# Two heads' inputs kept with zeros beside them, so that the state-space output products use the whole array

## The chip, the cores and the metric

The kernel runs on one core of one Trainium2 chip. The metric is the device time of one execution in microseconds (us). PE is TensorE, whose weight loads have a track of their own (PEld); DVE is VectorE, ACT is ScalarE, POOL is GpSimd, and SP issues the DMAs.

## The reference

Two layers of an encoder trunk over 512 tokens of width 1024 are computed, in float32. Each layer has three mixers on one projection, a gated sum of them, an output projection and an MLP. What the change touches is the state-space mixer (16 heads of 64 columns, 4 chunks of 128 tokens, one scan per direction):

```python
cb = jnp.einsum('bclgn,bcsgn->bcgls', Cm, Bm)
y_diag = jnp.einsum('bcghls,bcsghp->bclghp', cb[:, :, :, None] * decay, xdt)
w_state = jnp.exp(a_last[:, :, None] - a_cum)
states = jnp.einsum('bclgn,bclghp->bcghpn', Bm, xdt * w_state[..., None])
...
y_off = jnp.einsum('bclgn,bcghpn->bclghp', Cm, s_prev) * jnp.exp(a_cum)[..., None]
return (y_diag + y_off).reshape(Bsz, S, H, P)
```

The change is in `y_diag`: for each head and chunk, a 128x128 matrix of decays times the 128 tokens' 64 inputs. Both directions share one matrix M in the kernel, since their triangles are added first.

## The kernel before

The work runs through stages, each with its own buffers: norm (F), neighbourhood attention (N), gated linear attention (G), state space (S), and the MLP in the next F. Nearly all of PE's work is the large projections: `feat` makes one 128x512 output from 24 matmuls (lines 304 to 306: weights and inputs are each split in a high and a low part, three products for each of 8 blocks). Its output lies in one of two PSUM banks (`mm`, shown as `pf`), so a third `feat` starts only when the first one's bank has been read: by L592 (`gate`), L606 (`branch`), L777 (`conv_tile`) or L957 (`gate_tile`), all on DVE.

The G stage has float32 products of 256 columns, some written alone (L731) and some added to what an earlier product wrote (L748).

The S stage treats the 16 heads in 8 pairs. For a pair, `pair_prep` transposes the inputs (L880), copies them to `xt` (L882, ACT), weights them (L887, POOL) and builds the two heads' matrices M: two rows of sums are broadcast by DMA (`S_E`, `S_eB`), DVE takes their minimum (L898, four instructions a head), ACT takes the exponential (L903), DVE adds the two triangles (L904) and multiplies (L905). `pair_states` makes the states (L916, L922, L923). `pair_out` makes the output products `py` (L933), and adds them to the inputs (L934) with the states' part (L944, L945, POOL L947).

In `pair_out` each of the 4 chunks has two products, one for each head: 128 tokens contracted, 64 output rows, 128 output columns. Head 0 writes partitions 0 to 63 of `py`, head 1 partitions 64 to 127. A float32 product like this shows as two matmul instructions in the trace, so a pair has 16 and both layers have 256.

Between the pairs' steps, `fill` puts projections of other branches (convolutions, gates, branch outputs) in program order. The order on each engine is then set by a scheduler that plans with modelled times; it also moves single products away from their neighbours. Each engine runs its own instructions in that order.

Of the kernel before, what the change touches and what calls it, by code (L numbers as in the profile page):

```python
# [11 lines left out]
AF = mybir.ActivationFunctionType  # L12
# [4 lines left out]
P = 128  # L17
NT = 512
# [181 lines left out]
def trunk(tc, a, out, layers=L, dbg=None):  # L200
    nc = tc.nc
    V, S, G, T = nc.vector, nc.scalar, nc.gpsimd, nc.tensor
    with ExitStack() as ctx:
# [29 lines left out]
        def flat(ap):  # L233
            return ap.rearrange("p a b -> p (a b)")
# [20 lines left out]
        ph = Phase(tc, "F0", F_SB, F_PS)  # L255
# [41 lines left out]
        def feat(l, key, rh, rl, ps=None):  # L297

            hi, lo = wget(l, key)
            if ps is None:  # L300
                ps = psm("pf")
            for k in range(KT):
                c = slice(P * k, P * (k + 1))
                T.matmul(ps, lhsT=hi[:, c], rhs=rh[k], start=k == 0, stop=False)  # L304
                T.matmul(ps, lhsT=hi[:, c], rhs=rl[k], start=False, stop=False)  # L305
                T.matmul(ps, lhsT=lo[:, c], rhs=rh[k], start=False, stop=k == KT - 1)  # L306
            return ps
# [74 lines left out]
        for l in range(layers):  # L382
# [36 lines left out]
            if l:  # L419
                for j in range(KT):  # L420
# [5 lines left out]
            ph = Phase(tc, f"N{l}", {"s": 5, "pT": 4, "va": 2, "vb": 2, "bias": 5, "qA": 2, "qB": 2, "v": 2,  # L426
                                     "kA": 2, "kB": 2, "lA0": 1, "lA1": 1, "lB0": 1, "lB1": 1, "ebc": 1},
                       {"sc": 2, "pt": 2, "po": 1, "v": 1})
# [11 lines left out]
            for t in range(8):  # L440
                ps = feat(l, ("nk", t), xh, xl)
# [27 lines left out]
            for t in range(8):  # L469
                ps = ph.p("sc")  # L470
# [117 lines left out]
            def gate(b, j):  # L588
                ps = feat(l, ("gate", b, j), xh, xl)
                g_ = evac("gl")  # L590
                with hp():
                    V.tensor_tensor(g_, ps, rbc, ALU.mult)  # L592
                with hp():
                    S.activation(g_, g_, AF.Tanh, scale=0.5)
                return g_

            def branch(b, j, bh, bl, g_=None):
# [9 lines left out]
                if b:  # L607
# [4 lines left out]
            ph = Phase(tc, f"G{l}", {"A": 1, "kwT": 2, "st0": (3, 256), "st1": (3, 256), "t1": 3, "t2": 3, "w": 2,  # L612
                                     "gvg": 8, "bs": 2, "gst": 1, "q": 1, "k": 1, "a2": (2, 256), "kx": (2, 256)},
                       {"ga": 1, "at": 1, "x": 2, "po": 2})
            ps = feat(l, ("sm", 0), xh, xl)
# [181 lines left out]
            for h in range(1, 4):  # L797
                y = gla_mix(h, *cur)
                if h < 3:
# [4 lines left out]
            ph.close()  # L804


            ph = Phase(tc, f"S{l}", {"xt": 2, "bt": 1, "gs": 1, "xw": (2, 768), "st": (2, 768), "eb": 4, "E": 4, "eB": 2,
                                     "T": 2, "tb": 1, "sm": 2, "xs": 4, "bc": 1, "tm": (1, 256)},
                       {"x": 4, "py": 2})

# [28 lines left out]
            for d in range(2):  # L839
                r = slice(16 * d, 16 * d + 16)  # L840
# [19 lines left out]
            def ssd_group(g, t6):  # L860
# [11 lines left out]
                    V.copy_predicated(zt[d], trim[d], ps)  # L872
                return bt

            def pair_prep(g, j, t6):

                x_, r0 = t6[j], 8 * g + 2 * j
                ps = ph.p("x", (P, 4, P))
                for c in range(4):
                    T.transpose(ps[:, c], x_[:, P * c: P * (c + 1)], ident)  # L880
                xt = ph.t("xt", (P, 4, P))
                S.activation(xt, ps, AF.Copy)  # L882
                xw = ph.t("xw", (P, 2, 3, P))
                h2 = lambda ap: ap.rearrange("p c (h e) -> p c h e", h=2)
                for d in range(2):
                    w_ = wst[:, d: d + 3, 16 * d + r0: 16 * d + r0 + 2]
                    G.tensor_tensor(h2(xw[:, d]), h2(xt[:, d: d + 3]), w_.unsqueeze(3).to_broadcast((P, 3, 2, 64)),  # L887
                                    ALU.mult)
                M = []
                for hh in range(2):  # L890
                    rf, rb = r0 + hh, 16 + r0 + hh

                    ef, eb_ = ph.t("E", (P, 4, P)), ph.t("eB", (P, 4, P))
                    nc.sync.dma_start(flat(ef), acd[rf: rf + 1, :].to_broadcast((P, NT)))
                    nc.sync.dma_start(flat(eb_), acd[rb: rb + 1, :].to_broadcast((P, NT)))
                    t_, tb = ph.t("T", (P, 4, P)), ph.t("tb", (P, 4, P))
                    for c in range(4):
                        V.scalar_tensor_tensor(ef[:, c], ef[:, c], wj[:, c, rf: rf + 1], eb_[:, c], ALU.subtract, ALU.min)  # L898
                    for c in range(4):
                        S.activation(t_[:, c], zt[0][:, c], AF.Copy, scale=dt[:, c, rf: rf + 1])  # L900
                        S.activation(tb[:, c], zt[1][:, c], AF.Copy, scale=dt[:, c, rb: rb + 1])
                    for c in range(4):
                        S.activation(ef[:, c], ef[:, c], AF.Exp, bias=nab[:, c, rf: rf + 1])  # L903
                    V.tensor_tensor(t_, t_, tb, ALU.add)  # L904
                    V.tensor_tensor(ef, ef, t_, ALU.mult)  # L905
                    M.append(ef)
                return xt, xw, M

            def pair_states(g, j, bt, xw):

                r0 = 8 * g + 2 * j
                st = ph.t("st", (P, 6, P))
                for d in range(2):
                    ps = ph.p("x", (P, 3, P))
                    for c in range(3):
                        T.matmul(ps[:, c], lhsT=bt[:, d + c], rhs=xw[:, d, c], start=True, stop=True)  # L916
                    S.activation(st[:, 3 * d: 3 * d + 3], ps, AF.Copy)
                he = lambda ap: ap.rearrange("p d (h e) -> p d h e", h=2)
                for n, prev, cur in ((0, st[:, 0::5], st[:, 1:5:3]), (1, st[:, 1:5:3], st[:, 2:4])):
                    tm = ph.t("tm", (P, 2, P))  # L920
                    de = dec[:, n].rearrange("p (d h) -> p d h", d=2)[:, :, r0: r0 + 2]
                    V.tensor_tensor(he(tm), he(prev), de.unsqueeze(3).to_broadcast((P, 2, 2, 64)), ALU.mult)  # L922
                    V.tensor_tensor(cur, cur, tm, ALU.add)  # L923
                return st

            def pair_out(g, j, t6, xt, M, st):

                x_, Ct, r0 = t6[j], t6[5], 8 * g + 2 * j
                py = ph.p("py", (P, 4, P))
                for c in range(4):  # L930
                    for hh in range(2):
                        r = slice(64 * hh, 64 * hh + 64)
                        T.matmul(py[r, c], lhsT=xt[:, c, r], rhs=M[hh][:, c], start=True, stop=True)  # L933
                V.scalar_tensor_tensor(x_, x_, cc(C_D + 4 * g + j), flat(py), ALU.mult, ALU.add)  # L934
                for d in range(2):
                    eb = ph.t("eb", (P, 3, P))
                    for hh in range(2):
                        r = 16 * d + r0 + hh
                        nc.sync.dma_start(flat(eb[64 * hh: 64 * hh + 64]),
                                          ead[r: r + 1, P - P * d: NT - P * d].to_broadcast((64, 3 * P)))  # L940
                    ps = ph.p("x", (P, 3, P))
                    for c in range(3):
                        co = c + 1 - d
                        T.matmul(ps[:, c], lhsT=st[:, 3 * d + c], rhs=Ct[:, P * co: P * (co + 1)], start=True, stop=True)  # L944
                    V.tensor_tensor(eb, ps, eb, ALU.mult)  # L945
                    xo = x_[:, P - P * d: NT - P * d]
                    G.tensor_tensor(xo, xo, flat(eb), ALU.add)  # L947
# [46 lines left out]
            pairs = [(g, j) for g in range(2) for j in range(4)]  # L994
            bts, cs = [ssd_group(0, c0)], [c0, c1]
            cur = pair_prep(0, 0, c0)
            fill(2)
            st = pair_states(0, 0, bts[0], cur[1])
            for n, (g, j) in enumerate(pairs):
# [8 lines left out]
                if nxt:  # L1008
                    st = pair_states(*nxt, bts[nxt[0]], new[1])
# [9 lines left out]
            gs = [gate(2, j) for j in range(5)]  # L1019
# [6 lines left out]
            ph = Phase(tc, f"F{l + 1}", F_SB, F_PS)  # L1026
# [6 lines left out]
            for j in range(8):  # L1033
                ps = feat(l, ("wo", j), mh, ml, ph.p("pf"))
# [4 lines left out]
            for q in range(4):  # L1039
                hh_, hl_ = [], []  # L1040
                for i in range(8):
                    ps = feat(l, ("f1", 8 * q + i), xh, xl, ph.p("pf"))
# [6 lines left out]
                for j in range(8):  # L1049
                    ps = feat(l, ("f2", q, j), hh_, hl_, ph.p("pf"))  # L1050
# [23 lines left out]
```

## Time and profile before

| | |
|---|---|
| median of 3 runs | 2468.46 us (2467.49 to 2468.6) |
| the profiled execution | 2469.9 us |
| its span, first to last instruction | 2468.1 us |
| PE busy | 2452.2 us (99%) |
| DVE busy | 1425.8 us (58%) |
| ACT busy | 1162.1 us (47%) |
| POOL busy | 393.3 us (16%) |
| granted TensorE clock, mean | 0.998 |

The profiled execution took 1.8 us more than its span, and 1.4 us more than the median. A busy PE means that some matmul was in the pipeline, so its share doesn't tell how fast the matmuls follow each other; that is read from their start times.

### The profile page before, as it was taken

Reading aid. Unit: us, or ns where it says so; the run is one execution under the profiler, and the core shown is the slowest. Engines: PE = TensorE matmul, PEld = TensorE weight load, DVE = VectorE, ACT = ScalarE, POOL = GpSimd, SP = SyncE. Lnnn points to the kernel's source line nnn. Section 1 sums busy time; section 2 is a strip of 40 time slices with the busy share of each in tenths; the row PEclk is TensorE's granted clock in tenths of the full one; section 3 lists DMA queues with packets and bytes.
Section 4 is the critical chain, followed back from the end, with each engine's and each line's share of the span. In section 5 each row is a group of like instructions: output and inputs, shape, how many; then the busy total and the mean of one; then the engine's idle time right before and its main releaser. Section 6 shows DMA issues by size and latency. Waiting matters only on the chain.

```text
span 2468.1 us, 32626 instructions
## 1 busy us (share of the span) xinstructions
PE 2452.2 (99%) x12656; PEld 2064.9 (84%) x12656; DVE 1425.8 (58%) x2148; ACT 1162.1 (47%) x2055; POOL 393.3 (16%) x333
## 2 busy tenths in 40 slices
PE   8999999999999999999999999999999999999999
PEld 7888889988788888888888888899878888888887
DVE  6776534587976554444447755345889665434443
ACT  4575435555855342332335654255568543422321
POOL 3132101112431110000122221011124312100000
PEclk9999999999999999999999999999999999999999
DMA  5221222223533322322332222222245333222232
GB/s 185 94 88 61 89 94 79 69 69 119 178 116 120 99 97 94 98 99 94 124 128 94 82 72 79 94 71 78 77 129 168 108 128 101 96 94 96 93 103 86
DMA packets 84603, 249.38 MB, mean 101 GB/s; under 512 B 9824, under 2 KB 15840, under 8 KB 84448
## 3 DMA queue, kind: packets, MB, share of 16 engines
q1 hardware_dynamic: 84016, 246.85, 30.5%
q8 instruction: 100, 1.64, 0.3%
q14 instruction: 55, 0.45, 0.1%
q10 hardware_dynamic: 432, 0.45, 0.1%
HBM read 242.80 MB, written 4.46 MB: 100 GB/s over the span
## 4 chain that ended last, share of the span: by engine, by line
PE 96%; DMA 2%; DVE 1%; ACT 1%; issue 0%; SPq 0%; DVEq 0%
PE pf L304 14%; PE pf L305 14%; PE pf L306 14%; PE F_pf L306 11%; PE F_pf L305 11%; PE F_pf L304 11%; PE pt L322 3%; PE pt L321 2%; PE pt L323 2%; PE N_po L569 2%; PE N_pt L562 1%; PE S_x L944 1%; PE G_at L699 1%; PE S_py L933 1%; PE G_at L700 1%; PE S_x L916 1%
## 5 line engine op out<-in xcount | busy, mean ns | idle before, releaser
L285 ACT ACTIVATE wh<-wr 128x1024 fp32r<-128x1024 f32 x378 | 400.2, 1059 | 938.7 <-PE F_pf L305 429.7
L287 DVE TENSOR_TENSOR wl<-wr,wh 128x1024 fp32r<-128x1024 f32 x378 | 485.7, 1285 | 188.4 <-ACT wh L285 186.6
L304 PE MATMUL pf<-xh,wh 128*128 128x512 f32 x1232 | 486.2, 395 | 7.6 <-DVE gl L592 3.7
L305 PE MATMUL pf<-xl,wh 128*128 128x512 f32 x1232 | 486.6, 395 | 0.7 <-DVE xl L349 0.7
L306 PE MATMUL pf<-xh,wl 128*128 128x512 f32 x1232 | 486.2, 395 | 0.0
L304 PEld LDWEIGHTS pf<-xh,wh 128*128 128x128 f32 x1232 | 232.2, 189 | 57.0 <-DVE gl L592 4.6
L306 PEld LDWEIGHTS pf<-xh,wl 128*128 128x128 f32 x1232 | 232.3, 189 | 49.5 <-issue 1.5
L305 PEld LDWEIGHTS pf<-xl,wh 128*128 128x128 f32 x1232 | 232.4, 189 | 48.9 <-issue 1.2
L304 PE MATMUL F_pf<-Ah,wh 128*128 128x512 f32 x640 | 248.4, 389 | 0.0
L306 PE MATMUL F_pf<-Ah,wl 128*128 128x512 f32 x640 | 247.8, 389 | 0.0
L305 PE MATMUL F_pf<-Al,wh 128*128 128x512 f32 x640 | 247.8, 389 | 0.0
L306 PE MATMUL F_pf<-xh,wl 128*128 128x512 f32 x512 | 200.1, 391 | 0.0
L305 PE MATMUL F_pf<-xl,wh 128*128 128x512 f32 x512 | 199.3, 389 | 0.0
L304 PE MATMUL F_pf<-xh,wh 128*128 128x512 f32 x512 | 199.3, 389 | 0.0
L1051 DVE TENSOR_TENSOR F_x<-F_x,F_pf 128x512 f32<-128x512 f32 x64 | 44.0, 688 | 205.6 <-PE F_pf L306 205.6
L322 PE MATMUL pt<-wl,xh 128*128 128x256 f32 x512 | 146.1, 286 | 0.0
L323 PE MATMUL pt<-wh,xl 128*128 128x256 f32 x512 | 145.9, 286 | 0.0
L321 PE MATMUL pt<-wh,xh 128*128 128x256 f32 x512 | 144.9, 284 | 0.0
L304 PEld LDWEIGHTS F_pf<-Ah,wh 128*128 128x128 f32 x640 | 120.2, 188 | 25.0
L305 PEld LDWEIGHTS F_pf<-Al,wh 128*128 128x128 f32 x640 | 120.1, 188 | 25.0
L306 PEld LDWEIGHTS F_pf<-Ah,wl 128*128 128x128 f32 x640 | 120.1, 188 | 24.8
L1044 DVE SCALAR_TENSOR_TENSOR F_v<-F_pf,rx 128x512 f32<-128x512 f32 x64 | 44.1, 691 | 159.5 <-PE F_pf L306 159.5
(313 smaller groups left out, 4257.1 us busy)
## 6 DMA issues: line engine op xcount, KB each, us to landing
wr<-pk SPq DMA_DIRECT2D x378, 512.0 KB, 3.3
N_bias<-bias SPq DMA_DIRECT2D x48, 256.0 KB, 2.9
S_E<-acd SPq DMA_DIRECT2D x32, 256.0 KB, 4.3
S_eB<-acd SPq DMA_DIRECT2D x32, 256.0 KB, 3.8
S_eb<-ead SPq DMA_DIRECT2D x64, 96.0 KB, 3.5
F_x<-xt SPq DMA_DIRECT2D x15, 256.0 KB, 5.2
xd<-F_x SPq DMA_DIRECT2D x8, 256.0 KB, 2.0
F_x<-xd SPq DMA_DIRECT2D x8, 256.0 KB, 4.8
```

Of the source, the lines that this page charges most:

```text
L285: S.activation(hi, raw, AF.Copy)
L287: V.tensor_tensor(lo, raw, f(hi), ALU.subtract)
L304: T.matmul(ps, lhsT=hi[:, c], rhs=rh[k], start=k == 0, stop=False)
L305: T.matmul(ps, lhsT=hi[:, c], rhs=rl[k], start=False, stop=False)
L306: T.matmul(ps, lhsT=lo[:, c], rhs=rh[k], start=False, stop=k == KT - 1)
L321: T.matmul(o, lhsT=rh[k][:, s], rhs=hi[:, c], start=k == 0, stop=False)
L322: T.matmul(o, lhsT=rh[k][:, s], rhs=lo[:, c], start=False, stop=False)
L323: T.matmul(o, lhsT=rl[k][:, s], rhs=hi[:, c], start=False, stop=k == KT - 1)
L562: T.transpose(pt[:, i, kb], s[:, i, P * kb: P * (kb + 1)], ident)
L569: T.matmul(po[r, P * cb: P * (cb + 1)], lhsT=vv[:, v0 + kb, r], rhs=ptS[:, i, kb], start=kb == 0, stop=kb == 1)
L1044: V.scalar_tensor_tensor(v_, ps, 0.0, rbc, ALU.max, ALU.mult)
L1051: V.tensor_tensor(xT[j], xT[j], ps, ALU.add)
```

## The change

The inputs of a pair no longer lie as 4 blocks of 128 columns (64 of head 0, 64 of head 1). Two fixed buffers of 1152 columns are set to zero once per layer, and the copy from PSUM writes head 0 to columns 128c to 128c+63 and head 1 to columns 576+128c to 576+128c+63 of chunk c. A slice of 128 columns from 128c is then head 0 with 64 columns of zeros behind it, and one from 512+128c is 64 columns of zeros with head 1 behind them. Each product now has 128 output rows, and the two heads' products are accumulated in the same part of `py`.

```diff
-            ph = Phase(tc, f"S{l}", {"xt": 2, "bt": 1, "gs": 1, ...
+            ph = Phase(tc, f"S{l}", {"xt0": (1, 1152), "xt1": (1, 1152), "bt": 1, "gs": 1, ...
...
+            xts = [ph.t(f"xt{i}", (P, 1152)) for i in range(2)]
+            for t_ in xts:
+                V.memset(t_, 0.0)
+            own = lambda z: z.rearrange("p (h q) -> p h q", h=2)[:, :, 0: NT].rearrange(
+                "p h (c e) -> p h c e", c=4)[:, :, :, 0:64]
...
-                xt = ph.t("xt", (P, 4, P))
-                S.activation(xt, ps, AF.Copy)
+                xt = xts[j % 2]
+                S.activation(own(xt), ps.rearrange("p c (h e) -> p h c e", h=2), AF.Copy)
...
+                xc = own(xt).rearrange("p h c e -> p c h e")
...
-                    G.tensor_tensor(h2(xw[:, d]), h2(xt[:, d: d + 3]), w_.unsqueeze(3).to_broadcast((P, 3, 2, 64)),
+                    G.tensor_tensor(h2(xw[:, d]), xc[:, d: d + 3], w_.unsqueeze(3).to_broadcast((P, 3, 2, 64)),
...
                 for c in range(4):
                     for hh in range(2):
-                        r = slice(64 * hh, 64 * hh + 64)
-                        T.matmul(py[r, c], lhsT=xt[:, c, r], rhs=M[hh][:, c], start=True, stop=True)
+                        k = NT * hh + P * c
+                        T.matmul(py[:, c], lhsT=xt[:, k: k + P], rhs=M[hh][:, c], start=hh == 0, stop=hh == 1)
```

The scheduler's order differs within the S stages alone, in both layers in the same way. On PE the output products of the first pair stood like this in the first layer, behind the last projections of the fill (a row is one product, so two instructions in the trace; numbers tell buffers apart):

```order
L305 MATMUL pf_6151<-xl_159,wh_5980 128x512
L306 MATMUL pf_6151<-xh_158,wl_5981 128x512
L304 MATMUL pf_6151<-xh_162,wh_5980 128x512
L933 MATMUL S_py_5473<-S_E_5254,S_xt_5225 64x128
L933 MATMUL S_py_5473<-S_E_5230,S_xt_5225 64x128
...
L944 MATMUL S_x_5486<-X_bc_5104,S_st_5358 128x128 x2
```

In the changed kernel (whose lines stand 9 further from the middle of `pair_prep` on: L942 for L933, L953 for L944, L907 for L898, L914 for L905), the same place reads:

```order
L305 MATMUL pf_6202<-Al_4231,wh_6086 128x512
L306 MATMUL pf_6202<-Ah_4230,wl_6087 128x512
L304 MATMUL pf_6202<-Ah_4239,wh_6086 128x512
L942 MATMUL S_py_5476<-S_E_5258,S_xt_23_5207 128x128
L942 MATMUL S_py_5476<-S_E_5234,S_xt_23_5207 128x128
...
L953 MATMUL S_x_5489<-X_bc_5104,S_st_5362 128x128 x2
```

The products have 128 rows, as many of them as before; the projection in front is one `feat` further on. In both kernels the pair's first product stands alone some places ahead, and the other seven here.

On DVE the queue at the first two pairs' matrices stood so before (`gl` is a gate or a branch output, whose operation frees a PSUM bank for `feat`):

```order
L606 SCALAR_TENSOR_TENSOR gl_5897<-gl_5897,pf_5934 128x512
L898 SCALAR_TENSOR_TENSOR S_E_5230<-S_E_5230,S_sm_5157,S_eB_5231 128x128 x4
L904 TENSOR_TENSOR S_T_5234<-S_T_5234,S_tb_5235 128x512
L898 SCALAR_TENSOR_TENSOR S_E_5254<-S_E_5254,S_sm_5157,S_eB_5255 128x128 x4
L287 TENSOR_TENSOR wl_5981<-wr_5978,wh_5980 128x1024
L905 TENSOR_TENSOR S_E_5230<-S_E_5230,S_T_5234 128x512
L898 SCALAR_TENSOR_TENSOR S_E_5385<-S_E_5385,S_sm_5157,S_eB_5386 128x128 x4
L904 TENSOR_TENSOR S_T_5258<-S_T_5258,S_tb_5259 128x512
L898 SCALAR_TENSOR_TENSOR S_E_5409<-S_E_5409,S_sm_5157,S_eB_5410 128x128 x4
L922 TENSOR_TENSOR S_tm_5369<-S_st_5358,S_sm_5157 128x256
L592 TENSOR_TENSOR gl_6009<-pf_5984,rx_213 128x512
```

And so in the changed kernel:

```order
L907 SCALAR_TENSOR_TENSOR S_E_5234<-S_E_5234,S_sm_5158,S_eB_5235 128x128 x4
L785 SCALAR_TENSOR_TENSOR X_bc_5691<-cu_5689,col_120,X_bc_5691 128x510
L907 SCALAR_TENSOR_TENSOR S_E_5258<-S_E_5258,S_sm_5158,S_eB_5259 128x128 x4
L913 TENSOR_TENSOR S_T_5238<-S_T_5238,S_tb_5239 128x512
L287 TENSOR_TENSOR wl_6087<-wr_6084,wh_6086 128x1024
L914 TENSOR_TENSOR S_E_5234<-S_E_5234,S_T_5238 128x512
L907 SCALAR_TENSOR_TENSOR S_E_5388<-S_E_5388,S_sm_5158,S_eB_5389 128x128 x4
L907 SCALAR_TENSOR_TENSOR S_E_5412<-S_E_5412,S_sm_5158,S_eB_5413 128x128 x4
L606 SCALAR_TENSOR_TENSOR gl_6010<-gl_6010,pf_6090 128x512
L913 TENSOR_TENSOR S_T_5262<-S_T_5262,S_tb_5263 128x512
L931 TENSOR_TENSOR S_tm_5373<-S_st_5362,S_sm_5158 128x256
```

The first sum of triangles (L904, now L913) has moved behind the second head's minimum (L898, now L907), and the operation that frees the bank is now L606 and stands directly behind the second pair's minima.

## Rows read from the trace of the kernel before

**Rows 1.** The page, busy time of each engine: span, and PE's row.
```profile
span 2468.1 us, 32626 instructions
PE 2452.2 (99%) x12656; PEld 2064.9 (84%) x12656; DVE 1425.8 (58%) x2148; ACT 1162.1 (47%) x2055; POOL 393.3 (16%) x333
```

**Rows 2.** Groups on PE: shapes, count, busy us, mean ns, idle before.
```profile
L944 PE MATMUL S_x<-X_bc,S_st 128*128 128x128 f32 x192 | 28.6, 285 | 0.0
...
L933 PE MATMUL S_py<-S_E,S_xt 128*64 128x128 f32 x256 | 23.1, 289 | 1.7 <-DVE S_E L905 1.7
...
L731 PE MATMUL G_x<-G_gvg,G_kwT 128*128 128x256 f32 x64 | 16.4, 379 | 0.0
...
L748 PE MATMUL G_po<-G_st,G_t 128*128 128x256 f32 x48 | 14.3, 379 | 0.0
```

**Rows 3.** Timeline of PE, 717.9:723.5: start us, length us, instruction, count.
```profile
717.63 0.39 PE L305 MATMUL pf<-xl,wh 128*128 128x512 f32 x1
...
719.22 0.39 PE L306 MATMUL pf<-xh,wl 128*128 128x512 f32 x1
719.54 1.09 PE L933 MATMUL S_py<-S_E,S_xt 128*64 128x128 f32 x16
720.56 1.61 PE L944 MATMUL S_x<-X_bc,S_st 128*128 128x128 f32 x12
...
722.24 0.39 PE L305 MATMUL pf<-xl,wh 128*128 128x512 f32 x1
```

**Rows 4.** Timeline of PE, 700.2:703.8.
```profile
701.30 1.50 PE L916 MATMUL S_x<-S_xw,S_bt 128*128 128x128 f32 x12
...
702.87 0.40 PE L305 MATMUL pf<-Al,wh 128*128 128x512 f32 x1
```

**Rows 5.** Timeline of PE, 1848.1:1853.5, second layer.
```profile
1848.18 0.39 PE L304 MATMUL pf<-xh,wh 128*128 128x512 f32 x1
1848.50 1.09 PE L933 MATMUL S_py<-S_E,S_xt 128*64 128x128 f32 x14
1849.52 1.38 PE L944 MATMUL S_x<-X_bc,S_st 128*128 128x128 f32 x10
1850.74 1.50 PE L916 MATMUL S_x<-S_xw,S_bt 128*128 128x128 f32 x12
1852.17 0.43 PE L933 MATMUL S_py<-S_E,S_xt 128*64 128x128 f32 x2
...
1852.87 0.39 PE L306 MATMUL pf<-xh,wl 128*128 128x512 f32 x1
```

**Rows 6.** Waits of PE, whole span: us in total, times, longest us.
```profile
PE pf L304 <- DVE gl L592: 3.7, 2, 2.1
...
PE S_py L933 <- DVE S_E L905: 1.7, 2, 1.3
```

**Rows 7.** Timeline of PE at the first layer's first pair; in brackets, idle before.
```profile
616.87 0.43 PE L933 MATMUL S_py<-S_E,S_xt 128*64 128x128 f32 x2 [1.29 <-DVE S_E L905]
...
622.11 0.49 PE L304 MATMUL pf<-xh,wh 128*128 128x512 f32 x1 [2.08 <-DVE gl L592]
...
624.29 1.97 PE L933 MATMUL S_py<-S_E,S_xt 128*64 128x128 f32 x14
```

**Rows 8.** A window: length; PE, PEld, DVE, ACT, POOL busy (count); granted clock; DMA.
```profile
623.50:626.80 3.30, 3.30 (x20) 2.32 (x19) 3.27 (x6) 3.30 (x10) 0.00 (x0) 0.50 0.37 109
```

**Rows 9.** Timeline of DVE, 555:632.
```profile
561.48 1.41 DVE L349 SCALAR_TENSOR_TENSOR Al<-G_x,col,Ah 128x512 fp32r<-128x512 f32 x2 [2.23 <-ACT Ah L348]
...
613.93 1.14 DVE L898 SCALAR_TENSOR_TENSOR S_E<-S_E,S_sm,S_eB 128x128 f32<-128x128 f32 x4 [1.79 <-DMA S_eB<-acd]
...
621.38 0.68 DVE L592 TENSOR_TENSOR gl<-pf,rx 128x512 f32<-128x512 f32 x1
```

**Rows 10.** Groups on DVE.
```profile
L466 DVE MEMSET N_s<- 64x512 f32 x2 | 1.0, 485 | 0.3 <-issue 0.3
```

**Rows 11.** Groups on POOL, shapes apart.
```profile
L887 POOL TENSOR_TENSOR S_xw<-S_xt,S_sm 128x384 f32<-128x384 f32 x32 | 36.9, 1174 | 51.8 <-ACT S_xt L882 51.8
```

More of the change, by code (lines that the diff above doesn't have):

```diff
@@ L804, in trunk @@
             ph.close()
-            ph = Phase(tc, f"S{l}", {"xt": 2, "bt": 1, "gs": 1, "xw": (2, 768), "st": (2, 768), "eb": 4, "E": 4, "eB": 2,
+            ph = Phase(tc, f"S{l}", {"xt0": (1, 1152), "xt1": (1, 1152), "bt": 1, "gs": 1, "xw": (2, 768), "st": (2, 768), "eb": 4, "E": 4, "eB": 2,
                                      "T": 2, "tb": 1, "sm": 2, "xs": 4, "bc": 1, "tm": (1, 256)},
```

## The prediction, made before the run

> **What bounds the kernel.** The page comes first: PE is busy for 2452 of 2468 us [rows 1], so what the change is worth is what it does to PE's own work, plus the few places where PE stands still. The waits of PE [rows 6] name those places in the S stages: 3.7 us in two waits on `gl` L592 (2.1 and so 1.6) and 1.7 us in two on the matrix M, L905 (1.3 and 0.4), 5.4 us in all. The groups on PE say nothing of the change: a tiled product L933 has a mean of 289 ns and a full one of the same columns, L944, 285 ns [rows 2]. These are lengths from entry to end of a pipeline, and the reader should not use them as costs. Costs are read from the distance between starts, in the timeline.
>
> **The clockwork.** Seven `feat` matmuls start in 719.22 - 717.63 = 1.59 us [rows 3], so a step is 0.227 us. Twelve full 128x128 instructions (L916) start at 701.30, and two matmuls later it is 702.87 [rows 4]: 1.57 - 0.227 = 1.34 us, 0.112 us each. That is the price of an instruction that uses the whole array. The tiled products are cheaper: 16 of them start in 720.56 - 719.54 = 1.02 us [rows 3], 0.064 us each. So the two heads' halves, which write different partitions, do run beside each other before the change. But going into such a block and out of it costs something. From the `feat` matmul at 719.22 to the one at 722.24 it is 3.02 us; less two steps (0.454) and less twelve full instructions (1.34), the block of 16 cost 1.22 us, 0.20 us more than its starts span.
>
> **What it removes.** Per pair, 16 tiled instructions. The scheduler leaves them together in three of eight pairs of a layer, and in five it moves the first product (two instructions) away. [Rows 5] show such a pair's two pieces, 14 and 2: 1852.87 - 1848.18 = 4.69 us, less two steps (0.454) and 22 full instructions (2.46), is 1.77 us. So the second entry and exit cost 1.77 - 1.22 = 0.55 us more, and two pieces cost about what a full-array block would. One of the five pairs has a third piece in each layer; for it I add half of such an entry and exit up to the whole, 0.3 to 0.55 us. Both layers together: 6 x 1.22 + 10 x 1.77 + 2 x (0.3 to 0.55) = 25.6 to 26.1 us.
>
> **What it adds on PE.** 256 full instructions at 0.112 us are 28.7 us, wherever they stand: between `feat` matmuls a full block showed no price of entry beyond its 0.112 us each [rows 4]. What those rows don't show is two products that accumulate in one part of PSUM at this size. The `feat` matmuls accumulate at an even step [rows 3], and float32 products of 256 columns have the same mean, 379 ns, alone (L731) and accumulating (L748) [rows 2], so I take nothing for it. A bound above is half of the 0.20 us of an entry and exit, the smallest disturbance of PE that the rows show, on each of the 64 products of a second head: 6.4 us. A bound below for the whole would be the tiled rate, 0.064 us, if a full product were as quick as a half: 16.4 us. The nearest rows, full blocks of the same columns, say 0.112. Sum for PE: 28.7 - 25.6 to 26.1 = +2.6 to +3.1 us; I take 3.0.
>
> The Trainium skill speaks against the change more strongly. Its page "TensorEngine Tiling (Array Packing)", section "Theoretical Speedup", gives up to twice the throughput to products of 64 columns, and section "Key Properties" says that changing the tiling mode drains the engine. The pairs' starts (0.064 against 0.112 us) agree with the first, and the 0.20 and 0.55 us with the second. By the first alone the sum would be 28.7 - 256 x 0.064 = +12.3 us; by both it is the +3.0 of the rows.
>
> **What it adds elsewhere.** Two memsets of 1152 columns a layer. One of 512 columns takes 485 ns [rows 10]; by columns, 1.1 us each. They stand in DVE's queue just ahead of L349, where DVE was idle for 2.23 us, waiting for ACT [rows 9]: 2.2 us fit, and I take nothing. Without that cover all behind them on DVE is 2.2 us later, and if it reached PE whole, 4.4 us in both layers. The copy L882 and the weighting L887 read or write strides instead of runs of 128, with the same number of elements. POOL waited 51.8 us in all for L882 [rows 11] and PE didn't wait for either [rows 6], so nothing here, unless they become several times as long.
>
> **What moves.** The queue at the first pair. Before, PE stood for 1.29 us before the first product, then for 2.08 us before a new `feat` (bank not yet read by L592), and behind that the granted clock was 0.50, the 1.2 GHz level, between 623.5 and 626.8 [rows 7, 8]. A block of 14 took 1.97 us there and 1.09 at full clock [rows 5, 7]; half of 3.3 us, some 1.65, is what the drop cost. In the changed order the first sum of triangles stands behind the second minimum, which waited for a DMA until 613.93 [rows 9], so M is ready later by one such operation of 128x512, 0.68 us by [rows 9], and PE comes one `feat` matmul earlier (0.23): the first wait grows to some 2.2 us. The second wait is on L606 now. Two operations fewer stand ahead of it on DVE (L904 and L922, some 0.7 and 0.4 us), and PE comes to it four `feat` matmuls sooner after the first product, but starts those later. By the rows of layer 0: 616.87 + 0.7, then 2.0 us of work (3.16 before, less 4 x 0.227 and one exit) is 619.6; free at 622.11 - 1.0 = 621.1; a wait of 1.5. Together 3.7 where it was 3.4: a wash, +0.3 and +-1 a layer. The second layer's DMAs came sooner and it had 1.6 us there and no drop of the clock. I add 0.2 for both layers and leave the clock as it is. Queued behind those DVE instructions is everything that frees a bank, so PE is who waits for them.
>
> **Sum.** 3.0 + 0 + 0.2 = +3.2 us. On the profiled execution, 2469.9, that is 2473.1; it was 1.4 us above the median of its runs, so on the median 2468.46 it is **2471.7 us**, +0.13%. What a measurement of this kernel can tell from no change is about 0.2%, 4.9 us.
>
> **The rivals.**
> *The waits at the first pair grow (slower).* The place is L606 behind both minima of the second pair, which wait for two broadcasts queued on SP. If these land as late as in the first layer in both, PE stands about 2 us longer in the two layers together than I take, and the clock may fall in the second too, another 1.65 us: 3.0 + 2 + 1.65 = +6.7, 2475. It decides where PE's wait at the second layer's new `feat` comes above the 1.6 us it has now and the granted clock behind it is 0.5. For it: the first layer shows just that [rows 7, 8]. Against: the removed operations ahead of L606. Chance 0.20.
> *The memsets aren't covered (slower).* They wait for the G stage's last readers of the same memory; 4.4 us more would be +7.6, 2476. For it: 2.2 against 2.23 leaves no room. Against: DVE has further idle time and PE's banks are read with some us to spare there, as PE has no wait in [rows 6] at those lines. Chance 0.06.
> *The entries stay, or accumulating costs (slower).* If what looks like entry and exit belonged to float32 blocks and not to tiling, it would come back in the new order, and the sum would be the bare rates, +12.3: 2481. Against it, the full block of [rows 4] pays none. Chance 0.02, and 0.01 for the 6.4 us of accumulating (2478). The first is also what that page of the Trainium skill would give without its section on the drain.
> *The waits go away (still no change that shows).* All 5.4 us of waits and the 1.65 of the clock gone would make 3.0 - 7.05 = -4.0, 2464.4, not yet beyond 0.2%; half of it -0.5, 2468. Chance 0.15.
> *A full product is as quick as a half (faster).* 16.4 - 25.6 = -9.2 us, 2459. For it nothing but that accumulating pairs are not in the trace; against it all full blocks. Chance 0.03, and 0.02 for the waits and something else together.
>
> **How the numbers follow.** The forecast as it stands has 0.51. With the waits that go away it makes 0.66 for no change, and the slower rivals make 0.29; faster is 0.05. The range reaches from some waits gone (2467.5) to the slower rivals up to 2477; below lie the rest of that rival and the quick product, above the rate alone, and the ends hold 2 in 10.
>
> **What would show it.** In the profile after: L942 has 256 instructions of 128*128 and blocks of 16 start over 1.79 us, with a step of 0.112; no gap of 0.1 us on either side; the sum of PE's time in the S stages is 3 us longer per execution, some 1.5 in each layer. If a pair's starts are 0.064 apart, the price of the product was wrong; if they are over 0.13, accumulating costs. The memsets take 1.1 us each and L349 begins where it did, against the `feat` matmuls around it. A first wait of some 2.2 us and a second of some 1.5 in the first layer, and a granted clock of 0.5 behind them or not, tell of the queue. The prediction is wrong if the sum of PE's waits in the S stages moves by more than 2 us, or the clock falls once more or not at all.

## The result: 12 us slower, and the profile after

The changed kernel takes 2480.12 us (median of 5 runs, 2480.02 to 2481.27) where the kernel before takes 2467.85 (5 runs): ratio 1.0052, 95% interval 1.0039 to 1.0064, some 12 us. Forecast were 2471.7, with 2477 as the upper end. The profiled execution took 2481.27 us; its page begins so (busy us, share, instructions), beside [rows 1]:

```profile
span 2479.5 us, 32620 instructions
...
PE 2457.5 (99%) x12656; PEld 2079.0 (84%) x12656; DVE 1428.7 (58%) x2152; ACT 1162.2 (47%) x2055; POOL 388.3 (16%) x333
```

The span grew by 11.4 us, PE's busy time by only 5.3: the rest is time in which PE stands. First the products, in PE's timeline of after (start us, length us, instruction, count), beside [rows 3]:

```profile
695.63 0.40 PE L306 MATMUL pf<-Ah,wl 128*128 128x512 f32 x1
695.87 1.95 PE L942 MATMUL S_py<-S_E,S_xt 128*128 128x128 f32 x16
697.65 0.39 PE L953 MATMUL S_x<-X_bc,S_st 128*128 128x128 f32 x2
```

The 16 instructions start in 697.65 - 695.87 = 1.78 us, 0.111 each, and nothing stands on either side of them. The memsets and the weighting, in the groups on DVE and on POOL (count, busy us, mean ns, idle before), beside [rows 10, 11]:

```profile
L879 DVE MEMSET S_xt<- 128x1152 f32 x4 | 4.1, 1018 | 0.8 <-issue 0.8
```

```profile
L896 POOL TENSOR_TENSOR S_xw<-S_xt,S_sm 128x384 f32<-128x384 f32 x32 | 34.4, 1095 | 53.8 <-ACT S_xt L890 53.8
```

All of that is as forecast. What isn't is in the waits of PE. Over the whole span, the rows that belong to the S stages are these (us in total, times, longest), beside [rows 6]:

```profile
PE pf L304 <- DVE gl L606: 4.7, 2, 3.2
PE S_x L953 <- DVE S_st L932: 4.2, 7, 1.2
...
PE S_py L942 <- DVE S_E L914: 1.6, 2, 1.2
...
PE S_x L953 <- ACT S_st L926: 0.2, 1, 0.2
```

These come to 10.7 us, where [rows 6] had 5.4. PE's other waits all lie in the first 26 us of the kernel; they come to 7.0 us, where before had 6.3. The seven waits at L953, the states' part of the output, are new. At the first pair of the first layer PE now takes its first product without a wait for M that the profile shows, but stands 3.18 us before a `feat`, where it stood 2.08, and the half clock is behind that stand as it was in [rows 7, 8] (timeline of PE, then a window, whose last columns are granted clock, DMA share and GB/s).

```profile
622.51 0.46 PE L942 MATMUL S_py<-S_E,S_xt 128*128 128x128 f32 x2
...
628.18 0.50 PE L304 MATMUL pf<-Ah,wh 128*128 128x512 f32 x1 [3.18 <-DVE gl L606]
```

```profile
629.60:633.00 3.40, 3.40 (x14) 2.93 (x13) 3.40 (x6) 3.33 (x9) 0.28 (x1) 0.50 0.09 27
```

But all of this stands later. The S stage's chain begins with L813, goes through POOL's series for the softplus (L828, L829), PE's L854 and a DMA to DVE's first minimum. Of the kernel before, the start of PE's L854, and on DVE the first minimum L898 and the first finished output L934:

```profile
599.33 0.60 PE L854 MATMUL S_x<-con,S_sm 128*32 128x128 f32 x4
```

```profile
610.39 1.14 DVE L898 SCALAR_TENSOR_TENSOR S_E<-S_E,S_sm,S_eB 128x128 f32<-128x128 f32 x4 [3.23 <-DMA S_eB<-acd]
...
626.76 0.74 DVE L934 SCALAR_TENSOR_TENSOR X_xs<-X_xs,col,S_py 128x512 f32<-128x512 f32 x1
```

The same three of after (L854, L907, L943), and a stretch of POOL's timeline ahead of them:

```profile
606.65 0.60 PE L854 MATMUL S_x<-con,S_sm 128*32 128x128 f32 x4
```

```profile
616.32 1.14 DVE L907 SCALAR_TENSOR_TENSOR S_E<-S_E,S_sm,S_eB 128x128 f32<-128x128 f32 x4 [3.20 <-DMA S_eB<-acd]
...
634.75 0.74 DVE L943 SCALAR_TENSOR_TENSOR X_xs<-X_xs,col,S_py 128x512 f32<-128x512 f32 x1
```

```profile
591.11 0.53 POOL L829 TENSOR_SCALAR S_sm<-S_sm 128x128 f32<-128x128 f32 x1
592.93 1.29 POOL L608 TENSOR_TENSOR mixed<-mixed,gl 128x512 f32<-128x512 f32 x1 [1.29 <-DVE gl L606]
594.17 1.44 POOL L828 TENSOR_TENSOR S_sm<-S_sm 128x128 f32<-128x128 f32 x1
```

L854 is 7.3 us later. The span of after had lost 0.75 us by the start of the stage; six more `feat` matmuls (1.36 us) stand ahead of L813, and between L813 and L854 there are 158 where there were 135 (23 x 0.227 = 5.2 us; an expectation below says 24). PE waits for nothing there: what L854 reads was ready at 602.39, 4.3 us ahead of it, so its place in PE's order sets its time. On POOL a `branch` sum, L608, now stands inside the series and waits for DVE, and the series too ends 7.3 us later (596.78, before 589.46). So DVE's first minimum starts 5.9 us later, its first finished output 8.0 us later. What that does to DVE shows in one window that begins behind L854 of before, columns as in [rows 8]; of before, then of after:

```profile
600.00:705.00 105.00, 101.63 (x594) 83.77 (x593) 94.67 (x170) 87.20 (x237) 40.41 (x32) 0.98 0.56 172
```

```profile
600.00:705.00 105.00, 100.18 (x579) 86.52 (x579) 89.95 (x163) 84.46 (x229) 37.14 (x30) 0.98 0.56 164
```

DVE is busy 58% of the span but 94.7 of these 105 us. In after it has done 4.7 us less by 705 (at most 2 of them because the stage itself begins 2.1 us later). It has little idle time to make that up: from its first finished output to 705 it stands for 2.5 us in before and 3.8 us in after.

To compare kernels, each S stage (from its first L813 to its last L969) can be split by the distances between PE's starts: gaps that the profile calls waits; the extra at half clock; and what the products and changes of shape take beyond the plain steps of 0.227 and 0.112 us. Sums of both layers, us:

| kernel | median us | products and around them | waits | half clock |
|---|---|---|---|---|
| before | 2467.85 | 28.9 | 5.6 | 1.7 |
| after | 2480.12 | 34.7 | 10.9 | 1.6 |
| full products, order of before | 2473.01 | 32.1 | 5.2 | 1.7 |
| tiled products, order of after | 2477.56 | 32.4 | 12.9 | 0 |
| full, head of before, rest of after | 2468.25 | 32.3 | 3.5 | 0 |
| tiled, head of before, rest of after | 2465.62 | 30.3 | 2.1 | 0 |
| the same, each pair's products together | 2465.85 | 24.0 | 8.5 | 0 |

After's 34.7 holds some 2.5 us that its products don't take where few waits stand (32.1, 32.3). Around each of its waits PE loses some 0.3 us more than the gap that the profile calls a wait: 0.16 us or more ahead of it, and 0.10 in the first step behind it, at full clock too.

### The profile page after: what moved, and what is told of

Read it like the earlier page. It is cut to its first block, busy times and chain, and to the rows that moved or that the text cites. A ratio compares the mean times of both kernels' runs of the same rounds, so it can differ in the third digit from the quotient of the medians.

```text
span 2479.5 us, 32620 instructions
## 1 busy us (share of the span) xinstructions
PE 2457.5 (99%) x12656; PEld 2079.0 (84%) x12656; DVE 1428.7 (58%) x2152; ACT 1162.2 (47%) x2055; POOL 388.3 (16%) x333
## 4 chain that ended last, share of the span: by engine, by line
PE 94%; DVE 3%; DMA 1%; issue 1%; SPq 0%; ACT 0%; POOL 0%; DVEq 0%; POOLq 0%; ACTq 0%
PE pf L304 14%; PE pf L305 14%; PE pf L306 14%; PE F_pf L306 11%; PE F_pf L305 11%; PE F_pf L304 11%; PE pt L322 2%; PE pt L321 2%; PE pt L323 2%; PE N_po L569 2%; PE N_pt L562 1%; DVE S_E L907 1%; PE G_at L699 1%; PE G_at L700 1%; PE S_x L953 1%; PE N_sc L546 1%
## 5 line engine op out<-in xcount | busy, mean ns | idle before, releaser
L287 DVE TENSOR_TENSOR wl<-wr,wh 128x1024 fp32r<-128x1024 f32 x378 | 485.3, 1284 | 189.6 <-ACT wh L285 188.1
```

The source lines that it names most:

```text
L287: V.tensor_tensor(lo, raw, f(hi), ALU.subtract)
```

## The experiments

Most kernels here are held in a given order. A table of each engine's instructions in the S stages stands in the kernel, and each is made to follow the one before it, without a semaphore:

```python
for eng, (firsts, packed) in ORDER.items():
    ...
            rows = [seen[eng[:-1]][first + int(r)] for r in rel]
            for prev, i in zip(rows, rows[1:]):
                tc.add_manual_dep(i, prev.name, mybir.DependencyInfo(
                    mybir.DependencyClass.NoSync, mybir.DependencyReason.DATA), reason="order")
```

Its lines stand 10 further on: L942 of after is L952 in a held kernel, L933 of before is L943. No kernel was held in its own order unchanged, so the price of holding isn't shown by itself; the nearest to it, after's order with four operations a pair put together on DVE (below), took 2479.43 us where after took 2480.12. Ratios are to runs of the kernel before on the same chip (medians there 2468.1 to 2469.0).

**Products or order.** The changed kernel in the order of before, and the kernel before in the order of after.

```diff
+ORDER = { the rows of before }   # with the products of after
```

> The changed kernel (padded inputs, memsets, full-array products) with every engine's instructions in the S stages held in the order that the kernel before has there; the four memsets alone are free. Theory A, the order: the products cost some 3 us of PE and the other 8 to 9 us of the change come from waits that the scheduler's new order made (the second part of the states' product waits on L932 on DVE). Then this runs at 2468 + 3 = 2471 us (2470 to 2473), PE's waits on L932 are gone, and its waits in the S stages are those of before, some 5.5 us. Theory B, the load: wider products, memsets and strides make DVE late on queues that had nothing to spare, whatever the order. Then it stays at 2478 to 2481 and the waits on L932 are there.

Measured: 2473.01 us, ratio 1.0019 (1.0010 to 1.0028).

```diff
+ORDER = { the rows of after }    # with the products of before
```

> The kernel before (compact inputs, products of 64 rows) with every engine's instructions in the S stages held in the order of the changed kernel. Theory A, the order: the new waits stay, some 8 us, and the order cuts the tiled products into three more pieces a layer, 0.3 to 0.55 us each, so 2468 + 8 + 2 to 3 = 2478 to 2480 us, no quicker than the changed kernel itself. Theory B, the load: without memsets and full products the waits go, and it runs at 2468 plus the pieces, 2469 to 2472.

Measured: 2477.56 us, ratio 1.0036 (1.0024 to 1.0049). The waits of PE, first of the full kernel in the old order, then of the tiled one in the new:

```profile
PE pf L314 <- DVE gl L602: 4.3, 2, 2.3
...
PE S_py L952 <- DVE S_E L924: 0.7, 1, 0.7
```

```profile
PE S_x L954 <- DVE S_st L933: 6.6, 8, 1.2
PE S_py L943 <- DVE S_E L915: 3.2, 3, 1.9
PE pf L314 <- DVE gl L616: 3.1, 2, 2.2
```

The new waits go with the order and come without the change's own operations. Full products, memsets and strides together cost 4.5 us in the old order; the order alone costs 9.1 to the tiled kernel.

**Memsets and strides.** Full products from the compact inputs of before; this leaves out the separation of the heads, since each product takes both heads' columns. Once with the scheduler free, once in the order of before.

```diff
-                xt = xts[j % 2]
-                S.activation(own(xt), ps.rearrange("p c (h e) -> p h c e", h=2), AF.Copy)
+                xt = ph.t("xt", (P, 4, P))
+                S.activation(xt, ps, AF.Copy)
...
-                        T.matmul(py[:, c], lhsT=xt[:, k: k + P], rhs=M[hh][:, c], start=hh == 0, stop=hh == 1)
+                        T.matmul(py[:, c], lhsT=xt[:, c], rhs=M[hh][:, c], start=hh == 0, stop=hh == 1)
```

> Full-array products from the compact inputs: each head's matrix multiplies both heads' inputs, so the output leaves out the separation of the heads; no memsets, no strides, two accumulating products as in the changed kernel, the scheduler free. Theory A: 2468 + 3 us for the products and whatever waits its own new order has, read off the trace by PE's waits in the S stages; the step between its products is 0.112 us. Theory B in its memset form: without memsets the 8 us go, 2471; in its product form it stays at 2478 to 2481.

> The changed products (full array, both heads accumulate) held in the order of before as in the first of these runs, but read from the compact inputs of before: no memsets, no strides in the copy and the weighting. It leaves out the separation of the heads: each product takes both heads' columns. Against the 2473.0 of the full kernel in the old order it shows what memsets and strides cost. My step (they cost nothing): 2472 to 2474. If the four memsets of 1.1 us are not covered: 2469 to 2471.

Measured: 2478.27 (1.0027 to 1.0054) free, and 2472.08 (1.0008 to 1.0026) in the order of before. The second lies with the 2473.01 of the full kernel: memsets and strides cost nothing that can be told. The first is slow although its L854 starts at 598.56, early. Its scheduler made yet another order, and DVE's window shows the same shortage, 89.8 us, here from stands of 3.29 us before the minimum at 661.81 (a DMA) and 2.46 before L287 at 670.14:

```profile
600.00:705.00 105.00, 100.46 (x578) 86.43 (x577) 89.79 (x164) 83.99 (x230) 39.30 (x32) 0.98 0.55 169
```

So a late start is one way for DVE to lose time in this stage, not the only one.

**One operation's place.** In after's timeline of DVE, the four operations on a pair's states (L931, L932, twice) stand with others between them, and PE's L953 waits for the last. DVE, then PE:

```profile
683.66 0.43 DVE L932 TENSOR_TENSOR S_st<-S_st,S_tm 128x256 f32<-128x256 f32 x1
684.00 1.86 DVE L287 TENSOR_TENSOR wl<-wr,wh 128x1024 fp32r<-128x1024 f32 x1
685.79 1.05 DVE L931 TENSOR_TENSOR S_tm<-S_st,S_sm 128x256 f32<-128x256 f32 x1
686.76 0.68 DVE L913 TENSOR_TENSOR S_T<-S_T,S_tb 128x512 f32<-128x512 f32 x1
687.37 0.41 DVE L932 TENSOR_TENSOR S_st<-S_st,S_tm 128x256 f32<-128x256 f32 x1
```

```profile
687.83 1.16 PE L953 MATMUL S_x<-X_bc,S_st 128*128 128x128 f32 x8 [0.96 <-DVE S_st L932]
```

The reader is to see L287 (1.86) and L913 (0.68) ahead of what PE stands for. The next kernel puts the four together in every pair, for instance at the first:

```diff
 L931 TENSOR_TENSOR S_tm
+L932 TENSOR_TENSOR S_st
+L931 TENSOR_TENSOR S_tm
+L932 TENSOR_TENSOR S_st
 L914 TENSOR_TENSOR S_E
-L932 TENSOR_TENSOR S_st
 L287 TENSOR_TENSOR wl
-L931 TENSOR_TENSOR S_tm
 L592 TENSOR_TENSOR gl
-L932 TENSOR_TENSOR S_st
```

> The changed kernel in its own order on all engines, but on DVE the four operations on a pair's states (L931, L932, L931, L932) stand one behind the other, where 0 to 13 other operations stood between them. Nothing is left out. Theory A (the new order puts other operations of DVE, L287 and L913 among them, into the middle of the chain that PE's L953 waits for): most of the 4.2 us that PE waits at L953 for L932 goes, and about as much again of what follows those waits stays, so 2480.1 becomes 2475 to 2477. Theory C (PE comes to L953 too soon by its own new order, so that the chain's own length sets the wait, or what is put back on DVE makes PE wait at another line): 2479 to 2481, with the waits moved to L942 by L914 or L304 by L592 and L606.

Measured: 2479.43 us (1.0035 to 1.0060). Theory C: the waits at the states fell to 1.8 us, and those for M rose from 1.6 to 7.9:

```profile
PE S_py L952 <- DVE S_E L924: 7.9, 6, 2.2
...
PE S_x L963 <- DVE S_st L942: 1.8, 2, 1.0
PE pf L314 <- DVE gl L616: 1.7, 2, 0.9
```

My first account, that single operations stand at the wrong place in DVE's queue, fell with this. A reading that fits is that DVE as a whole is late, and which line PE waits at is a matter of who comes last; the next kernel tries it.

**The head of the stage.** In this kernel every engine does what it did in before up to PE's first product, and the rest in the order of after.

```diff
 ORDER = {
-    the rows of after
+    the rows of before up to PE's first S_py product (DVE: first L905, SP: fourth L895)
+    the rows of after that are left
 }
```

> The changed kernel, nothing left out. In each S stage every engine first does what it did, in the order of before, up to PE's first product with M (DVE up to the first L905, SP up to the fourth L895), and then all the rest in the order of after. In after, 24 more feat products and one more load of weights stand ahead of L854, which starts the stage's chain (step sizes to DMA to minimum on DVE); DVE's first minimum is 5.9 us later for it and its first finished output L943 8.0 us later than before. Theory H (this late start of DVE's work is what makes PE wait at later pairs, since DVE is busy without a break from there on): 2471 to 2474. Theory O (how DVE's and PE's later operations stand to each other makes the waits, wherever the chain starts): 2478 to 2481.

Measured: 2468.25 us, ratio 0.9997 (0.9988 to 1.0006): all of the 12 us are gone, with the changed products in place. Its waits of PE, and the window of above:

```profile
PE S_x L963 <- DVE S_st L942: 2.8, 4, 1.2
...
PE S_py L952 <- DVE S_E L924: 0.7, 1, 0.7
```

```profile
600.00:705.00 105.00, 103.56 (x605) 90.31 (x604) 95.80 (x171) 88.68 (x239) 42.37 (x32) 1.00 0.57 172
```

The chain starts early (L854 at 598.37, first minimum 608.41, first finished output 626.67), DVE gets 95.8 us done by 705, and PE has neither the stand at the first pair nor the half clock. That speaks for Theory H, but the time is 3 us below its range. M's product and PE's first product there, on DVE and on PE:

```profile
613.79 0.68 DVE L924 TENSOR_TENSOR S_E<-S_E,S_T 128x512 f32<-128x512 f32 x1
```

```profile
620.81 0.38 PE L952 MATMUL S_py<-S_E,S_xt 128*128 128x128 f32 x2
```

M is done 6.3 us before PE comes to it, where PE of before and of after took it within 0.1 us. In PE's timeline 81 `feat` matmuls stand between L854 and the first product; before has 53 and after 52. The first product keeps its place of after among the `feat` matmuls (6 + 158 + 52 = 135 + 81), and only the chain's start is 29 of them earlier. So against after this kernel tries the early start alone, while against before it also gives DVE a longer lead over PE. With that head and the order of before behind it the time was 2473.01; what the trace shows of these 4.8 us is the longer lead, with which the two stands at the first pair (4.3 us) and the half clock (1.7 us) are gone.

**What the change costs in that order.** The same order with the tiled products, and then with each pair's products brought together (in that order the trace has 16 pieces a layer, where 8 would do; the first of the two expectations takes them as whole, the second counts 18).

```diff
 ORDER = { head of before, rest of after }   # with the products of before
-    five pairs of a layer in two to four pieces on PE
+    each pair's eight products together
```

> The tiled products of the kernel before, held in the order that brought the changed kernel to 2468.25 (every engine's operations up to PE's first product with M in the order of before, the rest in that of after; here no pair's products are taken apart, except the first pair's last ones if the order has them so). Nothing is left out. The two kernels then differ in the products, the memsets and the strides alone. By the prediction's prices 16 blocks of 1.22 us stand against 28.7 us, 9.2 us less: 2459 to 2460 if no wait of PE grows. Rival F (DVE is busy almost without a break in these stages, so PE's saved time comes back as waits for it): 2464 to 2468, with waits of PE in the S stages well above the 3.5 us of that run.

> The run before this one (tiled products, head of before, rest of after: 2465.6) with each pair's products brought together on PE: in its order five pairs of a layer stood in two to four pieces, 18 pieces in a layer where 8 would do. Nothing is left out. There PE's steps in and around the products came to 15.1 us a layer; in the run of the unsplit kernel in the order of before they came to 11.2. Theory (a piece's entry and exit are PE's own time): 7 to 8 us less on PE, 2458 to 2460 if no wait grows. Rival F (what PE saves comes back as waits for DVE): 2463 to 2466, with waits of PE in the S stages of 5 us or more, where that run has 2.1.

Measured: 2465.62 (0.9979 to 0.9997) and 2465.85 (0.9979 to 0.9997). The first lies in Rival F's range but lacks its sign: its waits are 2.1 us, not above 3.5. What it paid was the pieces, with 30.3 us for products and around them. Between the two PE's own steps fell by 6.3 us (30.3 to 24.0) and the waits rose by 6.4 (2.1 to 8.5), all at one line:

```profile
PE S_x L954 <- DVE S_st L933: 8.5, 8, 1.7
```

So the second shows Rival F: what PE saves comes back as waits for DVE. Against the tiled kernel the changed one costs 2.6 us in this order.

**The split products and the first pair, in the order of before.** Three runs on what the prediction took for the tiled blocks and for the first pair: the tiled kernel with each pair's products together; this and DVE's L592 moved up to where DVE was idle at the first pair; and that move alone in the changed kernel.

```diff
 L898 SCALAR_TENSOR_TENSOR S_E   # first head
 L904 TENSOR_TENSOR S_T
+L592 TENSOR_TENSOR gl
 L898 SCALAR_TENSOR_TENSOR S_E   # second head
...
 L922 TENSOR_TENSOR S_tm
-L592 TENSOR_TENSOR gl
```

> The kernel before, held in its own order on all engines, but on PE the first product of a pair that stands 18 to 38 products ahead of the others (ten pairs; in two of them the last one apart too) is put back beside them. Nothing is left out. By the prediction's sum a second entry into and exit from the tiled products costs 0.55 us a pair and a third 0.3 to 0.55: ten pairs and two third pieces, 6.1 to 6.6 us less, 2468.5 becomes 2462 to 2463, if no wait of PE grows. Rival D (the pieces stand where PE would have waited, or PE's later arrival at the block is made up by waits for banks on DVE): 2466 to 2469, with waits of PE at S_py or pf above the 5.4 us of before. Rival E (entry and exit have no price beyond the starts): 2468.

> The kernel before in its own order with two things moved: the first products of ten pairs beside the others (as in the run of that alone, 2465.6), and DVE's L592 at the first pair ahead of the second minimum. Nothing is left out. In the run of the first alone PE waited 3.5 and 2.4 us for L592 and the clock fell to half behind both (1.7 us each). If these go and PE waits for M for up to 2 us a layer instead: 2459 to 2463. If the wait for M is as long: 2465 to 2466.

> The changed kernel held in the order of before, with one operation a layer moved: DVE's L592, which reads the bank that PE's feat product at the first pair waits for, stands behind the first sum of triangles L904, ahead of the second minimum (where DVE was idle for a DMA), and no longer 12 operations later. Nothing is left out. If that wait (2.3 and 2.1 us, with the half clock behind it in one layer, 1.65 us) goes and about 2 us of waiting for M come in its place in each layer at most: 2473.0 becomes 2467 to 2471. If the wait for M is as long as the one removed: 2472 to 2474.

Measured: 2465.62 (0.9981 to 0.9999), 2465.58 (0.9978 to 0.9996), and 2470.41 (1.0000 to 1.0018). In the first, products and what is around them took 22.4 us where before took 28.9: 6.5 less, in the range that the price of entries and exits gave. But only 2.5 us came out, nearest to Rival D: PE stood longer at the first pair, and the clock fell to half in both layers (3.4 us, where before had 1.7).

```profile
PE pf L314 <- DVE gl L602: 5.9, 2, 3.5
```

With L592 early that wait is gone, and waits at four other lines have come, 6.8 us in all: no gain. In the changed kernel the same move gave 2.6 us.

**The other head first.** The kernel before, scheduler free, with the heads' products exchanged, so that a pair's first product needs the M that is made second.

```diff
-                    for hh in range(2):
+                    for hh in (1, 0):
```

> The kernel before with the two heads' products issued in the other order (head 1, whose matrix is ready last, first), the scheduler free. No product can then run ahead of the other seven: of ten split pairs two stay split. If the price of entry and exit that the rows of before showed (0.55 us for a second piece, and 0.3 to 0.55 for a third) is right, PE saves 8 x 0.55 + about 1 = 5.5 us: 2462.5 if the order makes no new waits. By theory A the order's waits may move by several us either way, so 2458 to 2468; by theory B they stay and it is 2461 to 2464.

Measured: 2466.71 us, ratio 0.9994 (0.9985 to 1.0003), above what theory B allowed and within the range of theory A; products and around them took 23.4 us, 5.5 less than before, and waits with the half clock 9.7, 2.4 more.

## Why the prediction was wrong

The step that failed is "What moves", with its "I add 0.2 for both layers". The working of the other steps held. M's last operation on DVE for the first pair, of before and of after:

```profile
616.12 0.69 DVE L905 TENSOR_TENSOR S_E<-S_E,S_T 128x512 f32<-128x512 f32 x1
```

```profile
621.74 0.68 DVE L914 TENSOR_TENSOR S_E<-S_E,S_T 128x512 f32<-128x512 f32 x1
```

- **What it removes and adds on PE: right.** A full product is 0.111 us, accumulating costs nothing, no entry or exit is left. In the order of before, products and surroundings went from 28.9 to 32.1, +3.2 us, where +3.0 was taken. The time rose by 4.5 there, of which the table's sums show 2.8 (39.0 against 36.2), and by 2.6 in the order with an early head. The entry and exit of a tiled block were priced rightly too, as the 6.5 us of the unsplit kernel show.
- **What it adds elsewhere: right.** A memset is 1.02 us, L349 came 0.85 us later, of which 0.75 were lost before, and a kernel without memsets and strides lies within the noise of one with them.
- **What moves: wrong.** It looked at the queue of one pair and took everything ahead of it to start when it had started, so that M would be ready later by one operation of 0.68 us. M's L914 was done 5.6 us later (622.4 against 616.8, the ends of the two operations whose lines stand ahead of this list, of before and of after). The order had put 23 more `feat` matmuls between L813 and L854, and a `branch` sum into POOL's series; neither is among the prediction's rows. The first pair's waits did stay about the same in sum (4.7 us for two banks and 0.5 for M, where 3.7 and 1.3 stood), and the clock fell once, as forecast. But the sum came out by luck: in the first layer 2.2 us for M and 1.5 for the bank were forecast, and 0 and 3.2 were measured. The loss came behind it: 5.9 us of late start on an engine that is busy 94.7 of 105 us there come back as waits at later pairs. That the sum of PE's waits would move by more than 2 us was named as what would make the prediction wrong; it moved by 5.3, and what PE loses around its waits added some 2.5. With the 3.2 of the products these are the 11.0 us by which the table's sum for after (47.2) is above that for before (36.2).
- **The rivals.** None named this. "The waits at the first pair grow" had the right engine and the wrong place, and its sign failed: at the second layer's `feat` PE waited 1.54 us, at full clock. That PE has no wait in [rows 6] at DVE's other lines was read as some us to spare; the window of 94.7 us in 105 shows that there were few.
- **The Trainium skill.** What the Trainium skill's page "TensorEngine Tiling (Array Packing)", section "Key Properties", says of the drain at a change of the tiling mode agrees with the unsplit kernel: fewer changes of the tiling, 6.5 us less on PE. The bare rates, which are all that its section "Theoretical Speedup" speaks of, would have given 2481, near what came out; but the held kernels show that the products took 3.2 us of it, not 12.3.

What is shown: the order makes 9.1 us of it without the edit, and with the edit an early start of the chain, PE's first product keeping its place, takes the 12 us away. What stays open: after's head was not tried ahead of before's rest, nor after's rest at the shorter lead that before has, so it isn't told apart how much the late start costs by itself and how much the order behind it costs that a longer lead covers. Which of the moves in the head (the `feat` matmuls on PE, the load of weights on SP, L608 on POOL) would do it alone was not tried, since they were only moved together. That DVE's share of the stage sets the floor is argued from four tiled kernels at 2465.6 to 2465.9: their products took from 22.4 to 30.3 us, but products, waits and half clock together 31.9 to 33.3 in each; DVE's work itself was not made shorter.

## What to carry to other kernels

Where a scheduler plans the order, an edit to one operation can move the start of a whole stage. Before summing the edit's own cost, compare both orders from the stage's first instruction on, on every engine of its chain, and count what now stands ahead of each link.
Read the busy share of each engine by stage: DVE's 58% of the span was 90% in 105 us of the stage that was changed. There a saving of some 6.5 us on PE bought 2.5 us in one order and nothing in another, while a start of DVE's chain 29 `feat` matmuls (6.6 us) earlier in each of the two layers bought 12.
Holding a kernel in the other kernel's order takes the edit and the order apart, with one run for each.

## What was unexpected of the hardware

Whether the clock falls behind a stand of PE isn't told by the stand's length alone. In the run with the other head first PE stood 3.07 us in the first layer and 2.31 in the second, at the same place:

```profile
620.64 0.50 PE L304 MATMUL pf<-xh,wh 128*128 128x512 f32 x1 [3.07 <-DVE gl L592]
```

```profile
1842.83 0.49 PE L304 MATMUL pf<-xh,wh 128*128 128x512 f32 x1 [2.31 <-DVE gl L592]
```

The granted clock stayed at 2.4 GHz behind the longer one and was 1.2 GHz behind the shorter (windows behind each; the clock is the third number from the end):

```profile
620.60:624.00 3.40, 3.35 (x26) 2.51 (x26) 3.37 (x6) 3.40 (x11) 0.00 (x0) 1.00 0.35 101
624.00:627.40 3.40, 3.40 (x28) 3.27 (x27) 3.37 (x6) 3.40 (x11) 1.95 (x2) 1.00 0.81 266
1844.20:1847.60 3.40, 3.40 (x21) 2.35 (x19) 3.33 (x5) 3.40 (x10) 0.00 (x0) 0.50 0.40 104
```
